# Band attention scores: the matmul with k's low part contracts 128 rows over two copies of it, instead of 64

## The chip, the cores and the metric

The kernel runs on one core of a Trainium2 chip. The metric is the device time of one execution in microseconds (us); less is better. The time before is the median of three runs. A profile is one execution taken by the hardware profiler; its span goes from the first instruction to the last.

## What is computed

One step of a one-layer streaming encoder with three sub-layers: a mixer (band attention beside a convolution), cross-attention to a memory, and a feed-forward layer. There are 2048 new frames of one stream and 16 frames each of 8 running streams. The change lies in the band attention of the 2048 frames: 8 heads of 64, chunks of 64 frames, each of which attends to its own chunk and the 8 before it. Cut to what matters:

```python
q, k, v, ga, gb = jnp.split(xn @ w_in, ...)             # 512 columns each
s = jnp.einsum('bnqhd,bnkhd->bhnqk', qc, kb) * Dh ** -0.5  # Dh = 64, key band of 576
s = s + rel_bias(table, q_off, k_off)
s = jnp.where(key_valid, s, NEG_INF)
p = jax.nn.softmax(s, axis=-1)
o = jnp.einsum('bhnqk,bnkhd->bnqhd', p, vb)
```

## The kernel before

TensorE (PE) multiplies operands that are split in two: a number is a high part plus a low part, each exact in the format of the matmul. A product of split operands is high times high, high times low, and low times high. Nearly all work of the kernel is such products, three matmuls each (`mm3`).

The mixer handles the frames in four quarters of four tiles of 128 (`QT`; quarter 0 has the running streams' tile as well). For each quarter the input projection writes q and k, transposed and split, to scratch in device memory: `Qd` and `Kd` are [head, part, 64, token], part 0 high and part 1 low. The scale and a minus sign are folded into q. Besides, the convolution's 31 taps run on VectorE (DVE, L451), in an order that is stamped on DVE.

The band attention of a quarter (`attn`) goes over 8 heads, and in a head over 4 tiles of queries. For a head, `attn_load` issues five DMAs on SyncE's queue (SP): q into `aq`, all 128 rows, where rows 0 to 63 are the high part and rows 64 to 127 the low part; k into `ak` with two DMAs (L539: both parts into rows 0 to 63; L540: the high part again into rows 64 to 127); v into `av`; the bias into `ab`. So `ak` has two planes: plane 0 has k's high part twice, one copy above the other, and plane 1 has k's low part in the upper half alone. All these tiles have two buffers. Quarter 0 loads 4 key tiles to a head, the others 8.

`scores` handles one tile of 128 queries against its keys: 128, 256, 384, 512 or 640 of them (640 from the fifth tile on). The scores stand in `sc`, two banks of PSUM, one buffer. Up to 512 keys go in one block, 640 in two blocks of 320. For each block there are two matmuls: L562 contracts all 128 rows (q high and q low) with plane 0, which gives high times high and low times high; L563 contracts rows 0 to 63 (q high) with plane 1, which gives high times low. Then DVE adds the bias and takes the minimum (L567: `att`, and `amn` with the minimum), and ScalarE (ACT) takes the exponential into `apr` (L570). The transposes of the result (`xpose`, L584, copied by ACT at L586) run one piece later and the product with v (`values`, L596) two pieces later, so that PE has work in between.

The pieces of the mixer are put in order by `Plan`: each has a place on a common time line, written out in `PAR`, and attention of one quarter stands between projections of the next (quarter 3: between output projections). Each engine then takes its instructions in one order, in which the builder may move them against each other. Behind the mixer come the cross-attention and the feed-forward layer (`pu` and `pd`), which ends the program.

Of the kernel before, what the change touches and what calls it, by code (L numbers as in the profile page):

```python
# [20 lines left out]
P = 128  # L21
# [36 lines left out]
class Plan:  # L58
    """Pieces of the program, emitted in the order of their place on a common time line."""

# [13 lines left out]
class Kern:  # L74
# [13 lines left out]

    # ---- small helpers
    def split(self, hi, lo, src, scale=None, lo_eng=None):  # L90
        """src (times scale, a power of two) = hi + lo, each part exact in the matmul's format."""
        nc = self.nc
        if scale is None:
            nc.scalar.activation(hi, src, AF.Copy)  # L94
            return (lo_eng or nc.vector).tensor_sub(lo, src, fr(hi))  # L95
        else:
            nc.scalar.activation(hi, src, AF.Copy, scale=scale)
            return nc.vector.scalar_tensor_tensor(lo, src, scale, fr(hi), op0=ALU.mult, op1=ALU.subtract)
# [20 lines left out]
    def mm3(self, out, lhs, rhs, first, last):  # L119
        """out += lhs * rhs for split operands: lhs(a), rhs(b) give the part's AP."""  # L120
        for n, (a, b) in enumerate(PASSES):
            self.nc.tensor.matmul(out, lhs(a), rhs(b), start=first and n == 0, stop=last and n == 2)  # L122

    def norm_rows(self, pool, src, gain, bufs=2, x=None):
        """One tile of rows: rms-norm with gain, in f32 on chip."""
        nc = self.nc
        if x is None:
            x = pool.tile([P, D], F32, tag="nx", name="nx", bufs=bufs)
        nc.sync.dma_start(x, src)
        sq = pool.tile([P, D], BF16, tag="nsq", name="nsq", bufs=1)  # L130
        ss = pool.tile([P, 1], F32, tag="nss", name="nss")
        nc.scalar.activation(sq, x, AF.Square, accum_out=ss)  # L132
        r = self.rstd(pool, ss, 1, D, "n")
        nc.vector.scalar_tensor_tensor(x, x, r[:, 0:1], gain, op0=ALU.mult, op1=ALU.mult)  # L134
        return x

    def transpose_split(self, tp, x, dst):
        """The transpose of x [128, 1024], split; dst(q): where its k tiles 4q.. 4q+3 go (two APs [128, 4, 128])."""
        nc = self.nc
# [8 lines left out]
    def post_norm(self, pool, y, gain, res, dst, pn=False, xtag="xr", xbufs=2, end=False):  # L148
        """dst rows = res rows + rms-norm(y) * gain."""
        nc = self.nc  # L150
# [15 lines left out]

# [1 line left out]
    def mixer(self):  # L168
# [4 lines left out]
        with ExitStack() as st:  # L173
# [23 lines left out]
            def conv_weights():  # L197
                G["g"] = self.gain(vp, ["conv_ln_g"], "lng")
                G["b"] = self.gain(vp, ["conv_ln_b"], "lnb")
                # halved: x sigmoid(x) = (x / 2) (1 + tanh(x / 2))  # L200
                for t in (G["g"], G["b"]):
# [8 lines left out]

            # -- relative biases, negated: the scores are kept negated throughout
            # columns: the cached keys, then a window in which a stream's own new keys
            # lie at columns 240..255; sliced per stream, all others' keys are masked
            sbias = mc.tile([P, 480], F32, tag="sbias", name="sbias")
# [41 lines left out]

            # -- input projection ------------------------------------------------
            S = {}
# [30 lines left out]
            def load_w(q, c0, kh=None):  # L289
                """Columns c0.. of w_in: 128 of them for all rows, or 256 for the rows' half kh."""  # L290
                def f():
# [23 lines left out]
            def glu(q, c, gate, c0, n):  # L315
                def fn():
# [12 lines left out]
                    else:  # L329
                        u = U[q, c]  # L330
                        sg = mp.tile([P, 512], F32, tag="t512", name="sg")[:, :n]
                        # a sigmoid(g) = (a / 2) (1 + tanh(g / 2))
                        nc.scalar.activation(sg, pm, AF.Tanh, scale=0.5)
# [66 lines left out]
            def in_work(q, n):  # L400
                """The projection's pieces that use the n-th tile of weights."""
                if n < 8:
# [18 lines left out]

            # -- depthwise convolution -------------------------------------------
            def conv_in():
# [32 lines left out]
            def conv_state(q):  # L456
                """The rows of u that become the next step's conv buffers."""
                def fn():
# [20 lines left out]
            def conv_center(q, t):  # L479
                """Transposes a tile of the convolution's result and takes off the groups' means."""  # L480
                def fn():
# [45 lines left out]

            # -- band attention ---------------------------------------------------
            A, KQ, PEND, READY = {}, {}, [], []

            def attn_load(q, h):
                def fn():
# [5 lines left out]
                    kt = mp.tile([P, 2, 1024], F32R, tag="ak", name="ak")  # L538
                    nc.sync.dma_start(fr(kt)[0:HD, :, :nk * P], Kd[h, :, :, k0 * P:(k0 + nk) * P].rearrange("a d t -> d a t"))  # L539
                    nc.sync.dma_start(fr(kt)[HD:P, 0, :nk * P], Kd[h, 0, :, k0 * P:(k0 + nk) * P])  # L540
                    vt = mp.tile([P, 8, HD], F32, tag="av", name="av")
# [7 lines left out]
            def scores(q, h, i):  # L549
                def fn():  # L550
# [8 lines left out]
                    for b in range(nb):  # L559
                        o = sp[:, b, :w]  # L560
                        c = off + b * w
                        nc.tensor.matmul(o, qt[:, i * P:(i + 1) * P], kt[:, 0, c:c + w], start=True, stop=False)  # L562
                        nc.tensor.matmul(o, qt[0:HD, i * P:(i + 1) * P], kt[0:HD, 1, c:c + w], start=False, stop=True)  # L563
                    tt = mp.tile([P, 640], F32, tag="att", name="att")
# [56 lines left out]

            # -- sample streams' band attention -------------------------------------
            SA = {}
# [6 lines left out]
            def sattn_load(b):  # L630
                def fn():
# [7 lines left out]
                    qs = mp.tile([P, 4, 2, 16], F32, tag="a", name="qs")  # L639
                    # block-diagonal queries: column (h, q) is nonzero in its head's rows only  # L640
                    nc.gpsimd.memset(fr(Q), 0.0)
# [66 lines left out]

            # -- output projection --------------------------------------------------
            OP, ost = {}, ExitStack()  # L710
# [81 lines left out]

            # -- time line (units of tensor engine time) ------------------------------
            pl = Plan()
# [59 lines left out]

# [1 line left out]
    def wpiece(self, pool, src, name, bufs=6, to=None):  # L856
        """[128, 512] of a weight, split."""
        nc = self.nc
        s = pool.tile([P, 512], F32, tag="wst", name="wst", bufs=3)
        nc.sync.dma_start(s, src)  # L860
        w = pool.tile([P, 2, 512], F32R, tag="w", name=name, bufs=bufs) if to is None else to
        self.split(w[:, 0], w[:, 1], s)
        return w

    def sample_memory(self, ps, sp):
        """The sample streams' attention to their cached memories; leaves its transpose in self.oTs.
        Returns the pieces: (queries, attention)."""
        nc, I = self.nc, self.i
# [97 lines left out]
    def prompt_memory(self, ps):  # L966
        """Opens the pool for the prompt memory's keys and values; returns the pieces that prepare them."""
        nc, tc, I, mt = self.nc, self.tc, self.i, self.mt
# [42 lines left out]
    def memory(self):  # L1011
        """Cross-attention. For the prompt, whose memory is common to all tokens, the query projection is
        folded into the keys (M1 = Wq K^T) and the output projection into the values (Mo = V Wo)."""
        nc, tc = self.nc, self.tc
# [6 lines left out]
        with ExitStack() as st:  # L1021
            ps = st.enter_context(tc.tile_pool(name="ps2", bufs=1, space=PSUM, reuse_waits="tile"))

            # -- the prompt memory's keys and values
            oT = [mt.tile([P, 4, 2, P], F32R, tag="pr", name="oT") for _ in range(2)]
# [52 lines left out]

            # -- folding of the projections
            m1s = ExitStack()  # L1080
# [28 lines left out]

            # -- the prompt's tiles  # L1110
            XT, SC, PT = {}, {}, {}
# [107 lines left out]
class Ffn:  # L1219
    """Sub-layer 3, in blocks of tokens that stay on chip while all weights pass by."""  # L1220

# [6 lines left out]
    def open(self, ps):  # L1228
        """The part that starts while the layer before still ends: the first block's tokens and weights."""
        k = self.k  # L1230
# [85 lines left out]
    def run(self):  # L1316
        k, tc, mt = self.k, self.tc, self.mt
        blocks = self.blocks
        with self.sta, ExitStack() as st:
            self.ps = st.enter_context(tc.tile_pool(name="ps3", bufs=1, space=PSUM, reuse_waits="tile"))  # L1320
            k.tpb = 4
            # the banks of the last tile's values, still read, go to the transposes
            self.ps.tile([P, 512], F32, tag="tp", name="pt", bufs=4)
# [26 lines left out]
    def finish(self, gpost):  # L1350
        """The last tile's norm and residual, by halves."""
        nc, mt, k = self.nc, self.mt, self.k
# [36 lines left out]
```

## Time and profile before

| | |
|---|---|
| time, median of 3 runs | 3339.41 us (3328.83 to 3345.59) |
| the profiled execution, span from the first to the last instruction | 3340.9 us (no other time is listed for it) |
| PE busy | 3245.8 us, 97% of the span |
| weight loads (PEld) busy | 2744.1 us, 82%; they overlap PE |
| DVE busy | 1838.0 us, 55% |
| ACT busy | 1242.1 us, 37% |
| mean granted clock of PE | 0.980 |
| DMA | 417.87 MB, mean 125 GB/s |

A busy time is the time in which at least one of an engine's instructions ran. Matmuls are pipelined and their ends are modelled, so their starts tell more than their durations. The first scores start near 319 us, the last near 1064 us.

### The profile page before, as it was taken

Reading aid. Unit: us, or ns where it says so; the run is one execution under the profiler, and the core shown is the slowest. Engines: PE = TensorE matmul, PEld = TensorE weight load, DVE = VectorE, ACT = ScalarE, POOL = GpSimd, SP = SyncE. Lnnn points to the kernel's source line nnn. Section 1 sums busy time; section 2 is a strip of 40 time slices with the busy share of each in tenths; the row PEclk is TensorE's granted clock in tenths of the full one; section 3 lists DMA queues with packets and bytes.
Section 4 is the critical chain, followed back from the end, with each engine's and each line's share of the span. In section 5 each row is a group of like instructions: output and inputs, shape, how many; then the busy total and the mean of one; then the engine's idle time right before and its main releaser. Section 6 shows DMA issues by size and latency. Waiting matters only on the chain. (4 is left out here: it accounts for less than half of the span.)

```text
span 3340.9 us, 45210 instructions
## 1 busy us (share of the span) xinstructions
PE 3245.8 (97%) x16840; PEld 2744.1 (82%) x16840; DVE 1838.0 (55%) x2828; ACT 1242.1 (37%) x2509; POOL 615.1 (18%) x728
## 2 busy tenths in 40 slices
PE   7889999999999999999999999999999999999998
PEld 7787777878877788888887999988888888888887
DVE  6797988777633434533334544455445644455444
ACT  3233454434544434532223322233333433343332
POOL 4346252332212421021212000002000200010000
PEclk9998999999889999999999999999999999999999
DMA  5465665636654546512223322224333423333332
GB/s 179 125 177 147 195 169 150 167 105 164 193 148 138 173 152 198 173 55 73 60 78 121 116 77 75 79 93 148 101 101 98 158 95 101 101 121 127 97 101 73
DMA packets 313834, 417.87 MB, mean 125 GB/s; under 512 B 63368, under 2 KB 186256, under 8 KB 313542
## 3 DMA queue, kind: packets, MB, share of 16 engines
q1 hardware_dynamic: 305054, 384.04, 38.6%
q0 software_dynamic: 8560, 30.94, 2.3%
q8 instruction: 133, 2.18, 0.3%
q14 instruction: 87, 0.71, 0.1%
HBM read 349.26 MB, written 69.52 MB: 125 GB/s over the span
## 5 line engine op out<-in xcount | busy, mean ns | idle before, releaser
L122 PE MATMUL pu<-xT,wu 128*128 128x512 f32 (+1 forms) x3840 | 754.6, 358 | 3.1 <-DVE xT L95 2.5
L122 PE MATMUL pd<-wd,h 128*128 128x512 f32 x3264 | 750.1, 390 | 1.7 <-DVE y L1311 1.7
L122 PEld LDWEIGHTS pu<-xT,wu 128*128 128x128 f32 x3840 | 658.5, 188 | 95.5 <-DVE xT L95 2.7
L122 PEld LDWEIGHTS pd<-wd,h 128*128 128x128 f32 x3264 | 611.6, 188 | 129.2 <-DVE y L1311 2.1
L122 PE MATMUL pm<-xT,w 128*128 128x512 f32 (+3 forms) x1992 | 430.9, 368 | 12.8 <-POOL w L95 6.2
L451 DVE SCALAR_TENSOR_TENSOR acc<-u,wdT,acc 128x512 f32<-128x512 f32 x480 | 427.8, 891 | 6.3
L103 POOL TENSOR_SCALAR nm<-nss 128x1 f32<-128x1 f32 x103 | 31.7, 307 | 2026.0 <-ACT nsq L132 1080.9
L122 PEld LDWEIGHTS pm<-xT,w 128*128 128x128 f32 x1992 | 338.9, 195 | 58.8 <-POOL w L95 6.6
L94 ACT ACTIVATE wd<-wst 128x512 fp32r<-128x512 f32 x256 | 160.2, 632 | 422.8 <-PE pd L122 363.0
L95 POOL TENSOR_TENSOR w<-wst,w 128x512 fp32r<-128x512 f32 x154 | 221.7, 1453 | 350.2 <-ACT w L94 319.9
L1311 DVE TENSOR_TENSOR y<-pd,y 128x512 f32<-128x512 f32 x238 | 163.9, 689 | 203.4 <-PE pd L122 203.3
L1293 DVE SCALAR_TENSOR_TENSOR hh<-pu,r 128x512 f32<-128x512 f32 (+1 forms) x160 | 96.9, 609 | 321.8 <-ACT r L1292 321.4
L1292 ACT ACTIVATE r<-pu 128x512 f32<-128x512 f32 (+1 forms) x160 | 83.8, 528 | 365.9 <-PE pu L122 359.4
L95 DVE TENSOR_TENSOR wu<-wst,wu 128x512 fp32r<-128x512 f32 x256 | 171.6, 690 | 87.1 <-ACT wu L94 85.9
L122 PE MATMUL pm<-wo,cT 128*128 128x512 f32 x816 | 203.9, 400 | 0.0
L95 DVE TENSOR_TENSOR wd<-wst,wd 128x512 fp32r<-128x512 f32 x256 | 179.9, 727 | 33.3 <-ACT wd L94 32.6
L94 ACT ACTIVATE wu<-wst 128x512 fp32r<-128x512 f32 x256 | 157.9, 631 | 102.8 <-DMA wst<-w_ffn_up 66.6
L122 PE MATMUL y<-mo,pT 128*128 128x512 f32 x768 | 186.9, 398 | 0.0
L122 PE MATMUL sc<-m,xT 128*128 128x512 f32 x768 | 182.0, 393 | 0.3 <-ACT xT L94 0.3
L122 PEld LDWEIGHTS pm<-wo,cT 128*128 128x128 f32 x816 | 151.0, 189 | 31.5 <-issue 1.4
L122 PEld LDWEIGHTS y<-mo,pT 128*128 128x128 f32 x768 | 142.9, 188 | 33.0
L122 PEld LDWEIGHTS sc<-m,xT 128*128 128x128 f32 x768 | 143.0, 188 | 30.6 <-DVE xT L95 0.5
(246 smaller groups left out, 3900.1 us busy)
## 6 DMA issues: line engine op xcount, KB each, us to landing
wst<-w_ffn_up SPq DMA_DIRECT2D x256, 256.0 KB, 3.4
wst<-w_ffn_down SPq DMA_DIRECT2D x256, 256.0 KB, 3.0
wst<-w_in SPq DMA_DIRECT2D x160, 256.0 KB, 3.7
ak<-Kd SPq DMA_DIRECT2D x24, 512.0 KB, 5.5
ab<-biasd SPq DMA_DIRECT2D x32, 320.0 KB, 5.4
cx<-catd SPq DMA_DIRECT2D x17, 512.0 KB, 3.8
x1d<-oy POOLq DMA_DIRECT2D x17, 512.0 KB, 6.3
nx<-x1d SPq DMA_DIRECT2D x17, 512.0 KB, 3.8
```

Source lines behind the costliest of these rows:

```text
L94: nc.scalar.activation(hi, src, AF.Copy)
L95: return (lo_eng or nc.vector).tensor_sub(lo, src, fr(hi))
L103: nc.gpsimd.tensor_scalar(m, ss, 1.0 / count, EPS, op0=ALU.mult, op1=ALU.add)
L122: self.nc.tensor.matmul(out, lhs(a), rhs(b), start=first and n == 0, stop=last and n == 2)
L451: i = nc.vector.scalar_tensor_tensor(o, s, wdT[:, c, w:w + 1], o, op0=ALU.mult, op1=ALU.add)
L1292: nc.scalar.activation(r, pm, AF.Relu)
L1293: nc.vector.scalar_tensor_tensor(hh, pm, 0.0, r, op0=ALU.max, op1=ALU.mult)
L1311: nc.vector.tensor_add(y, pm, y)
```

## The change

The second DMA of k is made like the first: both parts into rows 64 to 127. Plane 1 of `ak` then has k's low part twice, as plane 0 has the high part. The second matmul contracts all 128 rows of q with plane 1, which gives high times low and, as a fourth product, low times low. The numbers of DMAs and of matmuls stay as they are. The rest of the diff takes out comments and docstrings (lines keep their count) and is cut here.

```diff
                     kt = mp.tile([P, 2, 1024], F32R, tag="ak", name="ak")
-                    nc.sync.dma_start(fr(kt)[0:HD, :, :nk * P], Kd[h, :, :, k0 * P:(k0 + nk) * P].rearrange("a d t -> d a t"))
-                    nc.sync.dma_start(fr(kt)[HD:P, 0, :nk * P], Kd[h, 0, :, k0 * P:(k0 + nk) * P])
+                    for j in range(2):
+                        nc.sync.dma_start(fr(kt)[j * HD:(j + 1) * HD, :, :nk * P], Kd[h, :, :, k0 * P:(k0 + nk) * P].rearrange("a d t -> d a t"))
...
                         o = sp[:, b, :w]
                         c = off + b * w
-                        nc.tensor.matmul(o, qt[:, i * P:(i + 1) * P], kt[:, 0, c:c + w], start=True, stop=False)
-                        nc.tensor.matmul(o, qt[0:HD, i * P:(i + 1) * P], kt[0:HD, 1, c:c + w], start=False, stop=True)
+
+                        for a in range(2):
+                            nc.tensor.matmul(o, qt[:, i * P:(i + 1) * P], kt[:, a, c:c + w], start=a == 0, stop=a == 1)
```

## Rows read from the trace of the kernel before

**Rows 1.** The page, part 1: busy us, share, instructions.
```profile
PE 3245.8 (97%) x16840; PEld 2744.1 (82%) x16840; DVE 1838.0 (55%) x2828; ACT 1242.1 (37%) x2509; POOL 615.1 (18%) x728
```
**Rows 2.** Busy time by stretch: length, engines (instructions), granted clock, DMA share, GB/s.
```profile
318.50:450.00 131.50, 125.83 (x766) 104.79 (x767) 121.62 (x202) 61.39 (x163) 40.65 (x32) 0.97 0.66 187
450.00:895.10 445.10, 433.87 (x2506) 355.22 (x2504) 337.21 (x502) 197.55 (x434) 153.59 (x125) 0.98 0.56 153
895.10:939.50 44.40, 42.34 (x142) 31.97 (x142) 22.13 (x38) 22.50 (x49) 7.15 (x11) 0.50 0.70 210
939.50:1065.00 125.50, 125.50 (x708) 101.28 (x707) 39.31 (x80) 58.63 (x143) 20.53 (x29) 1.00 0.41 118
```
**Rows 3.** Waits, 300 to 1070 us: us in total, times, longest.
```profile
DVE att L567 <- PE sc L563: 110.1, 64, 11.1
...
PE sc L562 <- DVE amn L567: 12.3, 8, 6.4
```
**Rows 4.** PE in order of time: start, us, what.
```profile
717.82 2.23 PE L122 MATMUL pm<-xT,w 128*128 128x512 f32 x9
719.89 0.31 PE L562 MATMUL sc<-ak,aq 128*128 128x320 f32 x1
720.13 0.41 PE L563 MATMUL sc<-ak,aq 64*128 64x320 f32 x1
...
721.16 0.77 PE L584 MATMUL tpa<-ident,apr 128*128 128x128 f32 x5
```
**Rows 5.** Groups by form, whole span: busy us, mean ns, idle before.
```profile
L122 PE MATMUL pu<-xT,wu 128*128 128x320 f32 x1536 | 227.4, 310 | 3.1 <-DVE xT L95 2.5 <-ACT wu L94 0.6
```
**Rows 6.** Weight loads in order of time, the same piece; idle before them in brackets.
```profile
719.66 0.19 PEld L562 LDWEIGHTS sc<-ak,aq 128*128 128x128 f32 x1
720.13 0.18 PEld L563 LDWEIGHTS sc<-ak,aq 64*128 64x128 f32 x1 [0.28 <-issue]
```
**Rows 7.** PE in order of time, a piece of quarter 0.
```profile
377.90 0.39 PE L562 MATMUL sc<-ak,aq 128*128 128x512 f32 x1
...
378.65 0.72 PE L122 MATMUL pm<-xT,w 128*128 128x512 f32 x2
```
**Rows 8.** The three later stretches, L562 alone: PE (instructions), PEld, clock, DMA.
```profile
450.00:895.10 445.10, 52.16 (x134) 25.55 (x134) 0.98 0.56 153
895.10:939.50 44.40, 10.57 (x17) 5.13 (x17) 0.50 0.70 210
939.50:1065.00 125.50, 16.52 (x42) 7.95 (x42) 1.00 0.41 118
```
**Rows 9.** PE in order of time, a piece at half clock and what follows.
```profile
921.39 0.61 PE L562 MATMUL sc<-ak,aq 128*128 128x320 f32 x1
...
923.62 2.39 PE L596 MATMUL oc<-av,apt 128*128 128x64 f32 x10
```
**Rows 10.** DMA issues, 300 to 425 us: count, KB each, median us to landing.
```profile
ak<-Kd SPq DMA_DIRECT2D x8, 256.0 KB, 5.4
ak<-Kd SPq DMA_DIRECT2D x8, 128.0 KB, 4.5
```
**Rows 11.** The page, part 6: DMA issues of the whole span.
```profile
ak<-Kd SPq DMA_DIRECT2D x24, 512.0 KB, 5.5
```
**Rows 12.** SP's queue in order of time: loads of k being issued.
```profile
348.94 0.68 SPq L540 DMA_DIRECT2D ak<-Kd  x1
...
885.60 0.58 SPq L539 DMA_DIRECT2D ak<-Kd  x1
...
892.90 0.51 SPq L540 DMA_DIRECT2D ak<-Kd  x1
```
**Rows 13.** PE in order of time: the first scores that use those loads.
```profile
354.56 0.22 PE L562 MATMUL sc<-ak,aq 128*128 128x128 f32 x1
...
904.60 0.61 PE L562 MATMUL sc<-ak,aq 128*128 128x320 f32 x1
```

## The prediction

> **What bounds the kernel now.** I began with the page's table of busy times, to see which engine has no room: PE is busy 97% of the span [rows 1]. The scores run only in the first third, so the second view was the busy time of each engine in four stretches: the heads of quarter 0 (318.5 to 450 us), those of quarters 1 and 2 with part of 3 (450 to 895.1), a stretch at half the granted clock (895.1 to 939.5), and the rest of quarter 3 (939.5 to 1065) [rows 2]. PE is busy 126 of 131, 434 of 445, 42 of 44 and 125.5 of 125.5 us; DVE comes next with 122, 337, 22 and 39. Third, the waits by releaser: in these 770 us the scores' first matmul waits 12.3 us for DVE's `amn` (L567, which reads the scores out of `sc`), while DVE waits 110.1 us for the scores (L563) [rows 3]. So PE paces this part, DVE follows, and DVE is close behind in quarter 0. What PE no longer spends should leave the end as long as DVE keeps up.
>
> A busy PE can still hide slack, since the ends of matmuls are modelled. So the fourth view is the order in time, read by starts alone [rows 4]. Nine 512-column matmuls of the input projection start 0.23 us apart (719.89 less 717.82, by 9). Then a 640-key piece of scores: its first matmul (L562, 128 rows, 320 columns) is followed after 0.24 us by the first of 64 rows (L563). From there to the transposes at 721.16 three matmuls take 1.03 us, 0.34 us each. The piece takes 1.27 us. Matmuls of 128 rows and 320 columns in the feed-forward layer, 1536 of them, take 227.4 us, 0.148 each [rows 5], and the program has as many weight loads as matmuls [rows 1]. The weight loads tell what is different: that of the piece's first matmul begins at 719.66, 0.23 us ahead of its matmul and under the one before; that of the 64-row matmul begins at 720.13, with its matmul, after an idle 0.28 us put down to "issue" [rows 6]. At each change between 64 and 128 rows nothing is overlapped.
>
> **The change part by part.** *The second matmul.* Its count, columns and accumulation stay; the operands become 128 rows high, so no change of height is left inside a piece, nor at its end (the transposes, values and projections around it have 128 rows). A 640-key piece has four matmuls and four changes. After: 4 x 0.148 = 0.59 us, so 1.27 - 0.59 = 0.68 us saved. A piece with up to 512 keys has two matmuls and two changes: from 377.90 to 378.65, 0.75 us, against 2 x 0.23 = 0.46 [rows 7]: 0.29 us. I take that for all 32 pieces of quarter 0, though the short ones may give less.
>
> How many pieces: L562 stands 134, 17 and 42 times in the three later stretches, two to a piece, so 67, 8.5 and 21 pieces [rows 8]; quarter 0 has 8 heads by 4 tiles, 32. In the half-clock stretch a piece takes 2.23 us (921.39 to 923.62) [rows 9]; with 0.148 doubled for half the clock, 4 x 0.296 = 1.18, and 1.05 is saved. The sum on PE:
>
> quarter 0: 32 x 0.29 = 9.3; quarters 1 to 3: 67 x 0.68 = 45.6; half clock: 8.5 x 1.05 = 8.9; the rest: 21 x 0.68 = 14.3; together 78.1 us.
>
> The ends for this price: nothing, if 128-row matmuls keep the 0.34 us here, and 78.1. I take the upper, since the 0.148 us row is nearest: same height, columns and kind of operands, and a load each. The first matmul of the piece itself is a witness: with 128-row work ahead of it, its load ran ahead.
>
> At this place a rule of the notes speaks against the change. The Trainium skill, "TensorE: Matmul & The Clock Gate", part 3, "What overlaps and what doesn't", says that a weight load overlaps matmuls in flight only when their row groups differ; after the change all groups are the same. By it each matmul would go on showing its load, 0.19 us on top of 0.148, 0.34 as now, and the sum would be nothing. The feed-forward row, 0.148 us with a load each, disagrees.
>
> *The loads of k.* Still two DMAs per head on SP's queue, issued at the same places; the second goes from one part to both, from 128 to 256 KB in quarter 0 and from 256 to 512 KB later: 8 x 128 + 24 x 256 KB, about 7.3 MB. Nothing is removed, so no gain. The first DMA already has the new size: in quarter 0 it lands in 5.4 us against 4.5 for 128 KB [rows 10], and the 512 KB ones in 5.5 [rows 11]. So a load lands at most some 0.9 us later. What covers it is the time between issue and use: a close one in quarter 0 is 5.6 us (348.94 to 354.56), one in the densest attention 11.7 (892.90 to 904.60) [rows 12, 13]. Later heads have 6 us to spare: zero. In quarter 0 a load could end the wait: at most 8 x 0.9 = 7 us. If that cover goes, the score waits on PE, and behind it in PE's order transposes, values and projection. I take it inside the reduction for quarter 0 below. Behind the longer DMAs on SP's queue stand v and bias of the same head; the queue spends 0.58 us on issuing a 512 KB one and 0.51 on a 256 KB one [rows 12], so they start less than 0.1 us later.
>
> *What goes through.* Quarter 0: DVE is busy 121.6 of 131.5 us, 9.9 us of room for 9.3, and in parts it has none; I let half through, 4.7. Quarters 1 and 2: DVE's 337 us in a stretch of 400 would be 84%; `sc` has one buffer, so each piece needs DVE to have read the one before, which stands behind convolution taps in DVE's order. I let nine tenths through, 41.0. Half-clock stretch: all, 8.9, DVE and ACT being half busy. The rest: all, 14.3, with DVE at 39 and ACT at 59 of 125. Together 68.9 us. Behind 1065 us PE stays the pace maker (97% over the whole span), and nothing is fixed in time, so what is won there is won at the end.
>
> The profiled span is 3340.9 us, 1.5 above the median of the runs; 3340.9 - 68.9 = 3272, on the median's scale **3271 us**, 2.0% faster. If nothing gets through in quarter 0 and six tenths in quarters 1 and 2: 27 + 8.9 + 14.3 = 50, 3289. If all of it does, 3261.
>
> **Rivals.**
> *The clock returns as well.* From 895.1 to 939.5 us PE ran at 1.2 GHz, granted 0.50 [rows 2], in a part of scores, transposes and values with little between; in the stretches beside it, with projections between, the same pieces ran at 0.98 and 1.00. With the matmuls closer together the clock may stay up here too. Half clock leaves 44.4 - 8.9 = 35.5 us of it; at full clock PE would need about half, but ACT is busy 22.5 us there and sets about 23. Another 12.5 us: 3258. Against it: what made the clock fall need not be PE's own.
>
> *DVE becomes the bound.* For: 92% busy in quarter 0, taps ahead of the scores in its order, PE's 12.3 us already waited for `amn`. Against: it waits 110 us for the scores itself, which shrinks first. Price: nothing from quarter 0 and half from quarters 1 and 2: 22.8 + 8.9 + 14.3 = 46, 3293.
>
> *The change doesn't do what it says.* The 0.34 us belong to the scores (their accumulation, their tiles), not to the height; then 3339, no change. For: only these matmuls show it. Against: L562 itself does not, after 128-row work. The page's rule on loads would end here as well.
>
> *Slower.* PE finishes pieces earlier, stands at the one `sc` buffer for DVE more often, and the clock falls to 1.2 GHz over the stretch 450 to 895.1, now granted 0.98. Each microsecond of work at half clock costs as much as the 0.148 us matmul doubled, so half of the time spent there; it decides once 138 us (69 / 0.5) run at half clock. With 200 us so: 3271 + 100 = 3371. For: the stretch at 0.50 lies in dense attention. Against: projections fill the stretch, and PE is idle 11 us of 445 in it.
>
> **How the numbers follow.** Forecast, 3261 to 3283: 0.47. Clock returns, about 3258: 0.20. DVE, about 3293: 0.20. No change: 0.08. Slower: 0.05. The first three are faster by over 0.5% (17 us, about what a measurement of this kernel can tell from no change): 0.87; within 0.5%: 0.08; slower: 0.05. The range takes in the forecast and most of the two cases beside it: 3250 to 3300. It also covers a few microseconds by which the builder may order the same instructions otherwise.
>
> **What the profile of the changed kernel would show.** Right: in the order in time the four matmuls of a 640-key piece start about 0.15 us apart and take 0.6 us instead of 1.27; their weight loads begin ahead of them, and the idle time put down to "issue" at L563's loads is gone. DVE's 110 us of waits for the scores shrink; the span from the first score to the last falls from 746 to about 678 us; the feed-forward layer starts some 70 us earlier and lasts as long. For the clock: no stretch of 40 us at 0.50. For DVE: PE's waits for `amn` grow to 30 us or more. Wrong: spacing stays at 0.34; or it falls, and the scores' first matmul waits for a DMA of `ak`; or the granted clock falls in quarters 1 and 2.

## The result and the profile after

The changed kernel takes 3285.84 us (median of 4 runs, 3282.68 to 3292.67), the one before 3338.43 us beside it; ratio on record 0.9851, 95% interval 0.9822 to 0.9879 (it is not the quotient of the two medians, 0.9842). That is 53 us less where 67 (3338 to 3271) were forecast, inside the range of 3250 to 3300. It lies between two of the cases that the range takes in, the forecast's own 3261 to 3283 and DVE's 3293, so the time alone doesn't tell them apart. The profiled span is 3287.0 us, 53.9 less than before.

First the step on which all hangs, PE in order of time in the changed kernel (start, us, what; both matmuls now stand at line 564):

```profile
706.37 0.74 PE L564 MATMUL sc<-ak,aq 128*128 128x320 f32 x4
706.95 0.71 PE L585 MATMUL tpa<-ident,apr 128*128 128x128 f32 x5
707.49 1.23 PE L597 MATMUL oc<-av,apt 128*128 128x64 f32 x10
708.53 0.83 PE L564 MATMUL sc<-ak,aq 128*128 128x320 f32 x4
709.19 0.63 PE L122 MATMUL pm<-xT,w 128*128 128x512 f32 x2
```

The four matmuls of a 640-key piece take 0.58 us from the first start to that of the transposes (706.95 less 706.37), where they took 1.27 [rows 4]; 0.145 us each. The weight loads of the same piece:

```profile
706.14 0.71 PEld L564 LDWEIGHTS sc<-ak,aq 128*128 128x128 f32 x4
```

They begin at 706.14, 0.23 us ahead of the first matmul, and run through without the idle time of [rows 6]. Over the whole attention, the idle time ahead of the scores' loads that is put down to "issue" was (us in total, times, longest; 300 to 1070 us before)

```profile
PEld sc L563 <- issue: 40.7, 213, 0.4
PEld sc L562 <- issue: 17.2, 95, 1.3
```

and is now 3.5 us. So the price of a 640-key piece was right.

Where did the rest go? The same four parts of the attention in both kernels, cut at the starts of four matmuls: the first scores, the first scores of quarter 1, the first piece of quarter 3's third head, and the output projection's first matmul; the last window ends with the last scores. Columns as in [rows 2]: length, busy time of PE, PEld, DVE, ACT, POOL, then granted clock, DMA share and GB/s. Before:

```profile
319.00:454.10 135.10, 129.07 (x782) 107.19 (x780) 124.21 (x206) 61.66 (x164) 40.65 (x32) 0.97 0.67 188
454.10:889.30 435.20, 424.81 (x2463) 348.89 (x2462) 328.75 (x487) 193.22 (x429) 151.32 (x123) 0.98 0.55 151
889.30:936.50 47.20, 44.68 (x158) 33.09 (x157) 25.46 (x45) 24.64 (x50) 9.42 (x13) 0.56 0.70 206
936.50:1065.00 128.50, 128.50 (x717) 103.69 (x717) 41.36 (x82) 60.53 (x147) 20.53 (x29) 0.99 0.42 121
```

After:

```profile
317.20:454.30 137.10, 122.12 (x767) 106.41 (x767) 119.57 (x207) 61.81 (x163) 44.00 (x34) 0.95 0.69 193
454.30:856.00 401.70, 378.48 (x2440) 341.24 (x2438) 331.93 (x484) 190.07 (x419) 149.85 (x119) 0.97 0.65 172
856.00:893.00 37.00, 26.33 (x170) 24.43 (x168) 24.99 (x40) 26.54 (x57) 12.32 (x15) 0.82 0.90 264
893.00:1008.00 115.00, 114.97 (x731) 103.36 (x731) 43.09 (x86) 60.37 (x146) 20.24 (x29) 0.99 0.57 161
```

The parts become 2.0 us longer and 33.5, 10.2 and 13.5 us shorter. PE's idle time (length less busy) goes from 6.0 to 15.0, from 10.4 to 23.2, from 2.5 to 10.7 and from 0 to 0. PE does what it did in less time and then waits. In quarter 0 all is given back, in the last part nothing. The waits tell for whom, in part (us in total, times, longest; 300 to 1070 us of the changed kernel, before in [rows 3]):

```profile
DVE att L568 <- PE sc L564: 62.9, 31, 10.0
PE sc L564 <- DVE amn L568: 24.8, 14, 7.2
PE oc L597 <- ACT apt L587: 7.3, 3, 3.1
PEld sc L564 <- issue: 3.5, 2, 2.1
```

PE waits 24.8 us for `amn` instead of 12.3, and DVE 62.9 us for the scores instead of 110.1: the two have come closer to being level. The waits for `amn` are half of the 48.9 us that PE idles in the four parts; the next longest is 7.3 us for ACT's copy of the transposes, ahead of the product with v. The longest wait for `amn` in quarter 0, DVE in order of time:

```profile
398.62 0.74 DVE L451 SCALAR_TENSOR_TENSOR acc<-u,wdT,acc 128x512 f32<-128x512 f32 x1
399.27 0.54 DVE L449 TENSOR_SCALAR acc<-u,wdT 128x512 f32<-128x512 f32 x1
399.85 3.11 DVE L451 SCALAR_TENSOR_TENSOR acc<-u,wdT,acc 128x512 f32<-128x512 f32 x4
402.88 0.28 DVE L568 CUSTOM_DVE_ANT_0 att<-sc,ab 128x128 f32<-128x128 f32 x1
```

and PE beside it:

```profile
398.18 0.33 PE L564 MATMUL sc<-ak,aq 128*128 128x128 f32 x2
398.35 0.33 PE L122 MATMUL pm<-w,xT 128*128 128x256 f32 x1
403.23 0.79 PE L564 MATMUL sc<-ak,aq 128*128 128x256 f32 x2 [4.55 <-DVE amn L568]
```

The scores of one tile are done at about 398.5; DVE reads them at 402.88, after six taps of the convolution that stand ahead in its order; the next tile's scores need the same buffer and start at 403.23.

The longer loads show as well. From issue to landing, median, after (DMA issues: count, KB each, us), to be held against 5.5 us in [rows 11]:

```profile
ak<-Kd SPq DMA_DIRECT2D x48, 512.0 KB, 7.1
```

### The profile page after: what moved, and what is told of

It reads as the page before. It is cut to its first block, busy times and chain, and to the rows that moved or that the text cites. A ratio compares the mean times of both kernels' runs of the same rounds, so it can differ in the third digit from the quotient of the medians.

```text
span 3287.0 us, 45183 instructions
## 1 busy us (share of the span) xinstructions
PE 3166.8 (96%) x16840; PEld 2731.9 (83%) x16840; DVE 1843.0 (56%) x2828; ACT 1243.1 (38%) x2509; POOL 620.8 (19%) x728
## 5 line engine op out<-in xcount | busy, mean ns | idle before, releaser
L451 DVE SCALAR_TENSOR_TENSOR acc<-u,wdT,acc 128x512 f32<-128x512 f32 x480 | 435.8, 908 | 6.4
L122 PEld LDWEIGHTS sc<-m,xT 128*128 128x128 f32 x768 | 142.9, 188 | 30.7 <-DVE xT L95 0.5
```

The source lines that it names most:

```text
L451: i = nc.vector.scalar_tensor_tensor(o, s, wdT[:, c, w:w + 1], o, op0=ALU.mult, op1=ALU.add)
```

## Experiments

Each ratio is against runs of the kernel before on the same chip; not all groups of experiments ran on one chip.

**The load alone** (`e1_load`).

```diff
-    nc.sync.dma_start(fr(kt)[HD:P, 0, :nk * P], Kd[h, 0, ...])
+    nc.sync.dma_start(fr(kt)[HD:P, :, :nk * P], Kd[h, :, ...])   # matmuls as before
```

> The kernel before with the longer second load of k alone; the second matmul stays at 64 rows and the copy of k's low part is not read. My theory (the change of height costs 0.34 us a matmul, the load nothing): 3338 us, within 0.3% of before, spacing 0.34 us in the scores. Rival (the load, or the order that the builder makes with it, takes part of the gain): 3345 to 3360 us.

3348.64 us; ratio 1.0047 (1.0032 to 1.0062). My theory's "nothing" is wrong: the load, or the order that the builder makes with it, costs 11 to 21 us where the matmuls stay. The order is not the same on any engine: on DVE some 600 lines of the list of instructions differ from that of before, and PE's, ACT's, GpSimd's and SP's differ too. No wait for `ak` is named in its trace. Its runs were granted 0.978 to 0.982 of TensorE's clock, those of before 0.979 to 0.987; at 0.979 the kernel before took 3339.81 us and this one 3348.38 and 3348.76. So part of the cost goes with a lower clock; whether the load lowers it is not shown.

**The matmul alone** (`e4_matmul`).

```diff
-    nc.tensor.matmul(o, qt[0:HD, ...], kt[0:HD, 1, c:c + w], start=False, stop=True)
+    nc.tensor.matmul(o, qt[:, ...], kt[:, 0, c:c + w], start=False, stop=True)
```

> The kernel before with the second matmul at 128 rows over plane 0, so that k's low part is left out of the scores and the loads of k are as before. The builder's order on DVE, ACT, GpSimd and SP is that of before. Theory that DVE alone takes back what is missing between 77 us on PE and 53 in the end: 3286 us, as the changed kernel. Rival, that the longer load or the new order takes it back: 3262 to 3270 us, and waits for amn as short as before (about 12 us).

3275.08 us; ratio 0.9822 (0.9804 to 0.9840), between the two numbers. PE waits for `amn` 23.1 us, about as in the changed kernel, so the rival's second half is out: DVE takes its part with the old loads too. The two kernels differ most in quarter 0, from the first scores to the first scores of quarter 1. First the load alone, then the matmul alone:

```profile
319.60:462.50 142.90, 135.56 (x767) 111.65 (x766) 118.28 (x206) 61.75 (x163) 39.78 (x34) 0.92 0.66 186
316.80:447.90 131.10, 121.12 (x782) 106.91 (x781) 123.01 (x206) 61.69 (x164) 42.66 (x32) 0.96 0.69 195
```

142.9 and 131.1 us, where the kernel before has 135.1 and the changed one 137.1. So the 128-row matmul alone gives 4.0 us in quarter 0, and the long load with its order takes more than that. To see whether the remaining 10 us of the whole are real, both ran again on one chip.

**Both again** (`again_change`, `again_oldload`).

> The change once more, with the kernel before untouched otherwise, beside the next run on one chip: 3286 us, ratio 0.985.

> The 128-row second matmul over plane 0 with the old loads (k's low part left out) once more. If the longer load, with the order it brings, takes part of the gain: 6 to 12 us under the run beside it. If the earlier difference was scatter: within 4 us of it.

3284.67 us, ratio 0.9851 (0.9828 to 0.9875), and 3279.22 us, ratio 0.9833 (0.9807 to 0.9859): 5.5 us apart, between the two expectations, with intervals that overlap. With the first pair the load's part is some 5 to 10 us, not settled. The clock has a hand in it: the runs with the old loads that were granted 0.981 and 0.984 took 3283.03 and 3282.61 us, no less than the change's at 0.982 and 0.983 (3282.43 to 3284.82); the two faster ones had 0.986 and 0.987. Quarter 0 comes out as in the first pair, 137.1 us with the long loads (granted 0.93) and 131.9 with the old ones (0.97).

**Two changes of height instead of four** (`e2_grouped`). The first matmuls of both blocks, then the second ones:

```diff
-    for b in range(nb):
-        matmul(128 rows, block b); matmul(64 rows, block b)
+    for b in range(nb):
+        matmul(128 rows, block b)
+    for b in range(nb):
+        matmul(64 rows, block b)
```

> The kernel before with the matmuls of a 640-key piece in the order 128, 128, 64, 64 rows instead of 128, 64, 128, 64: the same work, two changes of height instead of four, one copy of the low part. If each change costs: about 0.15 + 0.24 + 0.15 + 0.34 = 0.88 us a piece instead of 1.27, 96 x 0.39 = 37 us less on PE, of which some 25 reach the end: 3313 us. If the 64-row matmuls are slow whatever stands beside them: 64-row spacing 0.34 twice, 0.15 once for the first: about 1.1 us a piece, 96 x 0.17 = 16 us on PE and 3326 us.

3307.94 us; ratio 0.9921 (0.9904 to 0.9938). A piece in order of time:

```profile
709.90 0.45 PE L561 MATMUL sc<-ak,aq 128*128 128x320 f32 x2
710.28 0.55 PE L564 MATMUL sc<-ak,aq 64*128 64x320 f32 x2
710.76 0.77 PE L585 MATMUL tpa<-ident,apr 128*128 128x128 f32 x5
```

0.86 us (710.76 less 709.90) with the same four matmuls, as the theory of changes had it (0.88). Quarter 0 took 139.6 us here, although loads and order are those of before (135.1): single stretches of one profile can lie some us off.

**All at 64 rows** (`e3_all64`).

```diff
-    nc.tensor.matmul(o, qt[:, ...], kt[:, 0, c:c + w], start=True, stop=False)
+    nc.tensor.matmul(o, qt[0:HD, ...], kt[0:HD, 0, c:c + w], start=True, stop=False)
```

> The kernel before with both matmuls at 64 rows (q's low part is left out of the scores). If the change of height costs: 0.15 us between the matmuls of a piece, one change at its start and one at its end; about 0.24 + 0.15 + 0.15 + 0.34 = 0.88 us a piece of 640 keys, 3310 us. If 64 rows are slow by themselves: 0.34 us for every one, 1.36 us a piece, 3345 us or more.

3305.08 us; ratio 0.9912 (0.9895 to 0.9929). The piece:

```profile
707.75 0.85 PE L563 MATMUL sc<-ak,aq 64*128 64x320 f32 x4
708.52 0.77 PE L584 MATMUL tpa<-ident,apr 128*128 128x128 f32 x5
```

0.77 us for four 64-row matmuls, where the rival had 1.36. So 64 rows are not slow by themselves; changing between heights is. A piece's own time leaves out what a change costs just ahead of it or behind it. Counted from the start of the last projection matmul ahead to that of the second transpose, over the 13 or 14 pieces that stand between the two, the medians are 1.66 us with four changes (before), 1.27 and 1.26 with two (grouped, all 64), 0.92 with none (the changed kernel): 0.17 to 0.18 us a change in all three.

**Half of the taps** (`t_before`, `t_after`): in both kernels `range(1, 31)` of the taps becomes `range(1, 16)`.

> The kernel before with 16 of the 31 convolution taps (the others are left out, so the convolution's result is not the reference's). This only makes the pair with the next run: it takes about half of the tap time off DVE. No theory has a number for its own time; with DVE close behind PE in quarter 0, some 20 to 60 us under before.

> The changed kernel with the same 16 taps. Theory that DVE's taps take back the missing 24 us: the difference to the kernel before with 16 taps is 70 to 78 us, about all of PE's 77. Rival, that loads or order take it back: the difference stays near 53 us.

3313.83 us (0.9936, 0.9906 to 0.9966; 15 us under before by the medians, 21 by the ratio, at the low end of 20 to 60) and 3249.45 us (0.9745, 0.9714 to 0.9776): the change is worth 64 us here instead of 53. Each ratio's interval is some 10 us either way, so the 11 us between the two are not clear of noise. Busy times from the first scores to quarter 3's third head, cut as above, before with 16 taps:

```profile
313.60:436.40 122.80, 121.95 (x762) 101.99 (x760) 78.38 (x151) 63.12 (x164) 41.81 (x35) 1.00 0.75 206
436.40:859.30 422.90, 419.35 (x2463) 345.50 (x2461) 232.22 (x364) 191.94 (x426) 142.50 (x121) 0.99 0.57 155
```

and after with 16 taps:

```profile
313.40:434.30 120.90, 114.41 (x762) 101.94 (x761) 79.12 (x151) 62.42 (x164) 40.38 (x34) 0.99 0.78 213
434.30:817.40 383.10, 372.55 (x2440) 337.26 (x2439) 232.72 (x363) 188.22 (x416) 144.39 (x119) 0.99 0.67 180
```

Quarters 1 and 2 now give 39.8 us instead of 33.5, quarter 0 gives 1.9 instead of -2.0. PE's waits for `amn` are 13.7 us instead of 24.8 (300 to 1070 us). The taps seem to take back some, but not what I expected: in quarter 0 DVE is busy 79 of 121 us and PE still idles 6.5, which it did not before (0.9); 3.2 of these are waits for `amn`.

**The second copy by another queue** (`low_gpsimd`, `low_act`): the loads of before, and a third DMA.

```diff
+    nc.gpsimd.dma_start(fr(kt)[HD:P, 1, :nk * P], Kd[h, 1, :, ...])   # or nc.scalar
```

> The changed kernel, but k is loaded by the two DMAs of before and the second copy of the low part by a third DMA on GpSimd's queue. The bytes are those of the changed kernel; the builder's order on DVE is nearer to that of the kernel before (246 lines of difference instead of 601). If the order takes back the 10 us between the changed kernel and the one with the old loads: 3272 to 3278 us. If the bytes do: 3284 to 3288 us as the changed kernel.

> The same with the third DMA on ACT's queue (DVE's order: 283 lines of difference). Order theory: 3272 to 3280 us. Bytes theory: 3284 to 3288 us. ACT spends some 0.1 to 0.6 us a head on issuing, 3 to 20 us spread over 700 us in which it is half idle.

3285.46 us (0.9855, 0.9819 to 0.9891) and 3281.04 us (0.9835, 0.9801 to 0.9869). Neither can be told from the changed kernel, so neither theory is borne out. Quarter 0 took 133.3 and 130.3 us, with the bytes of the changed kernel (137.1). The profile of the second names one load that came late:

```profile
PE sc L563 <- DMA ak<-Kd: 6.1, 1, 6.1
```

**The plan shifted** (`taps_later`, `heads0_later`): `tb1, ta2, tb2, ta3, tb3` moved to 335, 355, 494, 520, 650; and `ae0` from 183 to 195.

> The changed kernel with the convolution's taps of quarters 1 to 3 placed later on the common time line (ends 335, 494 and 650 instead of 320.5, 480.2 and 642.5). If DVE's taps in front of the scores take back part of the gain in quarters 0 to 2, and later there is room: 3276 to 3282 us, PE's waits for amn under 20 us. If the waits are only moved: 3286 us.

> The changed kernel with the pieces of quarter 0's attention spread to 195 instead of 183 on the common time line. DVE theory: more room around each piece, 3280 us. Rival: no difference, 3286 us.

3286.52 us (0.9853, 0.9822 to 0.9883) and 3283.24 us (0.9843, 0.9814 to 0.9871): no difference from the change; PE's waits for `amn` are 26.4 and 26.1 us. The waits were moved, not removed. Quarter 0 took 132.1 and 133.4 us with the long loads, but the whole is no shorter beyond the noise.

## Why the prediction was right, and what was mis-sized

*The bound and the price.* Right: 0.58 us a piece against 0.59 forecast. That changes of height are the cause is shown by two kernels that make fewer of them with as many matmuls: 0.86 and 0.77 us. The Trainium skill, "TensorEngine Tiling (Array Packing)", section "Key Properties", has a sentence that may name it: changing the tiling mode, not just the tile, drains TensorE. It gives no price and doesn't say that 64 rows beside 128 are such a change; the runs show one that costs 0.17 to 0.18 us each, and not by what. The rule of the Trainium skill on weight loads that spoke against the change ("TensorE: Matmul & The Clock Gate", "What overlaps and what doesn't") does not hold here: loads of all 128 rows run ahead of 128-row matmuls (706.14 against 706.37). By parts, PE's busy time fell by 7.0, 46.3, 18.4 and 13.5 us, where the sum had 9.3, 45.6, 8.9 and 14.3: quarter 0's short pieces gave less than the 0.29 us taken for all, and the third part's 18.4 holds the clock's rise.

*What goes through.* This is the term that was mis-sized. Quarter 0: 4.7 us forecast, -2.0 measured. Quarters 1 and 2: 41.0 forecast, 33.5 measured. Half-clock part: 8.9 forecast, 10.2 measured, and that these agree is luck (see the clock). The rest: 14.3 and 13.5. From the first scores to the last it takes 690.8 us instead of the 678 forecast. With 1.8 us won ahead of the first scores (319.0 to 317.2) they make 57.0, of which 3.1 are lost behind the scores, where nothing was to be lost (granted clock 1.00 before, 0.99 now): 53.9. The lower case that I worked out, nothing in quarter 0 and six tenths in quarters 1 and 2, gave 3289; it was nearly that.

*DVE as the bound.* Half a rival. Its own sign, 30 us or more of waits for `amn`, was not reached: 24.8. That DVE's taps in front of the scores, with `sc` in one buffer, hold PE up is seen in the wait that ends at 403.23. How much they take back is not settled: with 16 of 31 taps the change is worth 64 us, 11 more than with all, at intervals of ten. They don't explain quarter 0, where PE idles 6.5 us with a DVE two thirds busy. I took busy shares over a stretch for room; the waits come from the order inside it.

*The loads of k.* Mis-sized: I forecast 0.9 us later in landing and nothing for later heads; the 512 KB loads take 7.1 us instead of 5.5, and the load alone makes the kernel 11 to 21 us slower, part of it with a lower clock. In the changed kernel its share is smaller, 5 to 10 us by two pairs, the second inside its scatter. I had left out that the builder's order follows the loads, on every engine. What quarter 0 lacks goes with the loads: with the old ones the 128-row matmul gives 4.0 and 3.2 us there, near the 4.7 forecast, with the long ones it loses 2.0 both times. No wait for `ak` is named with the load alone or in the changed kernel, the same bytes by another queue leave quarter 0 at 133.3 and 130.3 us, and shifted plans with the long load at 132.1 and 133.4; this speaks for the order, though with one profile each, and the grouped kernel's 139.6 us with old loads and order warns of scatter. Whether bytes or order cost the time stays open: no run here held the order and changed the bytes.

*The clock.* The forecast kept the half-clock part; the rival had it go. It went for the larger part: 0.56 became 0.82 granted in that part. But the gain was 10.2 us, as PE, now faster, idles 10.7 of 37.0 us there, and ACT and DVE are busy 26.5 and 25.0. The clock's gain turned into waits, so 3258 was not reached. The forecast's 8.9 us had another ground, half clock as before with all of the saving let through, so that it came near 10.2 is chance.

*No change, slower.* Both out. Over quarters 1 and 2 the granted clock is 0.97 (before 0.98). In quarter 0 it went from 0.97 to 0.95, and to 0.93 in the second profile of the change: there what "slower" feared is seen in small.

## What to carry to other kernels

A matmul that contracted fewer rows than its neighbours cost more here than one filled up with rows that add nothing needed: look at starts, not durations, and at whether its weight load begins ahead of it. If operands can't be filled up, put the matmuls of one height together; that alone won 25 us with no more data. And a saving on the engine that sets the pace reaches the end only as far as the next engine's order lets it: count its waits, stretch by stretch, rather than its busy share.

## What the runs showed that was not expected

The longer load of k, alone, made the kernel 0.47% slower (0.32 to 0.62) without a wait for it being named: with one DMA's size changed, the builder put the instructions of all engines in another order. Four matmuls of 64 rows with a change of height at either end take as long as two and two grouped (1.26 and 1.27 us with what stands beside them), where all of 128 rows take 0.92 and two and two alternating 1.66. And the time of one kernel goes with the clock that it is granted: on one chip the kernel before took 3341.63 us at 0.980 and 3324.27 at 0.988, so a few us between two kernels tell little unless their clocks are alike.
